# Two-layer hybrid diffusion trunk on one core: low parts of the choice stages on VectorE, attention two heads side by side

## The chip, the cores and the metric

The kernel runs on 1 core of one Trainium2 chip. The metric is the device time of one execution in microseconds (us). TensorE (PE) multiplies, VectorE (DVE), ScalarE (ACT) and GpSimd (POOL) work on the data between the multiplications, SyncE (SP) starts most transfers. All five run their own queue of instructions in order, and a semaphore holds an instruction until what it reads is there.

## The reference, cut to what matters

```
def reference(x, c, ctx, c_ctx, ...):
    lat, cx = x, ctx                                  # 256 latent and 256 context tokens, D = 1024
    for l in range(2):
        hl, hc = modulate(rms_norm(lat, ...)), modulate(rms_norm(cx, ...))
        yl, yc = even_mixer(...) if l % 2 == 0 else odd_mixer(...)
        lat = lat + gate * yl
        ff = peer(modulate(rms_norm(lat, ...)), w_q, b_q, sub_keys, u, v)   # layer 0: latent and context tokens
        lat = lat + gate * ff
    return lat

def sink_attention(q, k, v, sink, mask):              # in odd_mixer: 12 query heads of width 64, 4 key/value heads
    s = einsum(q, k) * 64 ** -0.5                     # 256 queries, 256 context keys and a window of latent keys
    p = softmax(concat([sink, where(mask, s, -inf)]))[..., 1:]
    return einsum(p, v)

def peer(h, w_q, b_q, sub_keys, u, v):                # per token, 8 heads
    q = h @ w_q + b_q                                 # 8 heads x 2 halves x 128
    s = einsum(q, sub_keys)                           # 128 keys for each half
    sv, si = top_k(s, 16)                             # for each half
    best, pos = top_k(sv[0][:, None] + sv[1][None], 16)
    gate, eidx = softmax(best), index of the pair     # 16 of 128*128 experts for each head
    act = gelu(einsum(h, u[eidx])) * gate
    return einsum(act, v[eidx])
```

All arithmetic is held to float32. The kernel gets there on the fast matmul type (fp32r) by splitting both operands into a high part (a copy rounded to fp32r) and a low part (the operand less its high part), with three matmuls for each product: high by high, high by low, low by high (`mm3`, L109, L110, L111).

## The kernel before, in words

The program is, for each of two layers, a mixer and an expert stage, run one after the other. Tile pools with a number of buffers for each tag carry the dependences; a scheduler of the tile framework orders the instructions of each engine's queue (outside the blocks ordered by hand, which lie in the dense stages and the first norm). What the order of the text says is thus not the order in a queue; the sections on order below show the queues.

**Mixer of layer 1** (about 1716 to 1871 us of the trace). Queries and keys of all heads are normalised and rotated by `heads` (L1062 on, buffers `hsq` and `hn`), transposed into `qt` (12 heads, two to a column of 128 partitions, 64 partitions each) and `kt` (four key heads, each on 64 of the 128 partitions, the other 64 rows zero, L1061 and L1115). For each head and half of the queries, `scores` (L1147 on) is one matmul of 128 x 512 over 128 rows (L1152; half of the rows are zeros in `kt`), a mask, a softmax on DVE and ACT; `flip` transposes the result (L1174) into `pt`; `values` (L1184 on) multiplies by `vt` into 64 columns of the array, four matmuls for each head (L1189), eight for a pair, of which the first four go to one half of the columns and the last four to the other. Scores run one step ahead of the transposes. Between these stand the modulation vectors of the same layer, `mod` (L161): groups of matmuls of which each uses 32 columns (L171).

**Expert stage** (`peer`, L499 on). A norm, then the choice of experts: for each of four blocks of `w_q` (two heads each) `wsplit` (L681 on) makes four high parts on ACT (L65) and four low parts (L73), three of them on POOL and the last on DVE, after the letters "ap ap ap av" (a = ACT, p = POOL, v = DVE). `evaluate` projects (L109 to L111, into `qp`), copies (L652), multiplies with the keys (L655, L661) and copies the scores out (`sc`, L657). `select` is DVE's: the two best eights of each 128 scores (L523 to L529), sums of pairs (L540, L543), the two best eights again (L549 to L555), the subtraction of the best (L557), then indices and a gather by comparison (L562 to L577). The softmax over all chosen ones (L581 to L585) ends the stage; its first instruction, an Exp on ACT (L581), needs L557 of the last head.

PE has room in this stage, and it is filled with the **first halves** of the dense stage after it: `spare(1)` after each head (L690) loads a block of `u`, makes its high part on ACT (L743) and its low part (`ul`, L748), multiplies (L109 to L111 into `mm`), applies a Gelu (L766) and stores the result. `prepare` and `spare` take the engine of the low part as an argument, POOL by default (L600 and L608). After the last head `spare(nq)` makes 2 more in layer 0 and 6 more in layer 1 (L694). Then come the gate-build (L789 to L820) and the dense loops, where the low parts are DVE's already. In the trace the choice of layer 0 lies at about 367 to 553.5 us (first selection at 399.5), that of layer 1 at about 1871 to 2003 us (first selection at 1895.4), and six first halves of layer 1 up to 2020.3 us.

Of the kernel before, what the change touches and what calls it, by code (L numbers as in the profile page):

```python
# [9 lines left out]
F32 = mybir.dt.float32  # L10
# [27 lines left out]
class Kern:  # L38
# [460 lines left out]
    def peer(self, l, halves, D0, nstash=0, nq=2, ng=(1, 1)):  # L499
# [11 lines left out]
        with ExitStack() as st:  # L511
# [107 lines left out]
            with ExitStack() as st2:  # L619
# [419 lines left out]
    def mixer1(self):  # L1039
        nc, i = self.nc, self.i  # L1040
        with ExitStack() as st:
            m = self.open(st, "m1")
            px = self.open(st, "m1ps", space=PSUM)
            aux = lambda shape: px(shape, F32, tag="aux", bufs=3)
            pj = lambda shape: px(shape, F32, tag="pj", bufs=3)
# [17 lines left out]
            def heads(x, nh, gain, out, rope):  # L1063
# [7 lines left out]
                n = m([128, nh, 64], F32, tag="hn", bufs=1)  # L1071
# [76 lines left out]
            def scores(c, o, t):  # L1148
                hd = 2 * c + o
                sk = rows[:, 128 + hd:129 + hd]  # L1150
                sp = pj([128, 512])
                nc.tensor.matmul(sp, qt[:, c, t * 128:(t + 1) * 128], kt[:, QPERM[hd] // 3], start=True, stop=True)  # L1152
                ob = 256 + (1 - t) * 128
                nc.vector.tensor_add(sp[:, ob:ob + 128], sp[:, ob:ob + 128], band[:, t])
                mx = m([128, 4], F32, tag="mx", bufs=4)
                nc.vector.tensor_reduce(mx[:, 0:1], sp, axis=AX.X, op=ALU.max)

                nc.vector.tensor_scalar(mx[:, 1:2], mx[:, 0:1], 0.125, sk, op0=ALU.mult, op1=ALU.max)
                nc.vector.tensor_scalar(mx[:, 1:2], mx[:, 1:2], -1.0, None, op0=ALU.mult)
                nc.scalar.activation(mx[:, 3:4], sk, AF.Exp, bias=mx[:, 1:2])  # L1160
                s = m([128, 512], F32, tag="s", bufs=3)
                nc.scalar.activation(s, sp, AF.Exp, bias=mx[:, 1:2], scale=0.125, accum_out=mx[:, 2:3])
                nc.vector.tensor_add(mx[:, 2:3], mx[:, 2:3], mx[:, 3:4])
                nc.vector.reciprocal(mx[:, 2:3], mx[:, 2:3])
                if t:
                    nc.vector.tensor_scalar(s, s, mx[:, 2:3], None, op0=ALU.mult)
                else:
                    nc.scalar.activation(s, s, AF.Copy, scale=mx[:, 2:3])
                return s
# [10 lines left out]
            steps = [(c, o, t) for c in range(6) for o in range(2) for t in range(2)]  # L1180
            S = {0: scores(*steps[0])}
            PT, OV = {}, {}

            def values(c, o):  # L1184
                kvh = QPERM[2 * c + o] // 3
                if o == 0:
                    OV[c] = self.mm([128, 256])
                for j in range(4):
                    nc.tensor.matmul(OV[c][64 * o:64 * o + 64], vt[:, j, 64 * kvh:64 * kvh + 64], PT[c][:, o, j], start=j == 0, stop=j == 3)  # L1189
                if o == 1:  # L1190
                    self.split(OV.pop(c), yh[:, c], yl[:, c])
                    for _ in range(2 if c in (1, 3) else 1):
                        self.mod(1, mods.pop(0))

            for n, (c, o, t) in enumerate(steps):
                if n + 1 < len(steps):
                    S[n + 1] = scores(*steps[n + 1])
                if (o, t) == (0, 0):
                    PT[c] = m([128, 2, 4, 256], F32, tag="pt", bufs=2)
                flip(S.pop(n), PT[c][:, o], t)  # L1200
                if t == 0 and n:
                    values(*steps[n - 1][:2])
# [117 lines left out]
```

## Time and profile before

| | us |
|---|---|
| median of 3 runs | 2738.8 (2738.1 to 2743.56) |
| the profiled execution, its own time | 2737.01 |
| its span in the trace | 2735.2 |
| PE busy | 2601.4 (95% of the span) |
| DVE busy | 2130.2 (78%) |
| ACT busy | 1382.1 (51%) |
| POOL busy | 656.0 (24%) |

Times of the trace are from the start of the span. What lies around the span is 1.8 us. "Busy" is the time in which an engine has an instruction in work, overlap counted once; a matmul's end is modelled, so a busy PE need not be at its peak. Shares of the whole span say little of a stage; the stages are looked at one by one, and in each the question is which engine has no idle time left, and what the others wait for. PEclk is the clock that TensorE was granted, as a share of 2.4 GHz.

### The profile page before, as it was taken

The page shows a single profiled execution, that of the slowest core. Times are in us where ns is not written, and L with a number is a line of the kernel's source. Part 1 is how long each engine was busy: PE and PEld are TensorE (multiplying, and loading weights), DVE is VectorE, ACT ScalarE, POOL GpSimd, SP SyncE. Part 2 cuts the span into 40 slices and gives each one's busy share as a digit, 9 for nine tenths or more (in the row PEclk, how much of TensorE's full clock was granted, in tenths as well). Part 3 has the DMA queues.
Part 4 walks back from the last instruction along what each step waited for, and adds up shares of the span by engine and source line. Part 5 has one row for each costly group of instructions (what it writes and reads, how often), then busy time and mean ns, then how long its engine had stood idle before and what let it go on. Part 6 is the DMA issues. An engine that isn't in the chain of part 4 may idle for free.

```text
span 2735.2 us, 40202 instructions
## 1 busy us (share of the span) xinstructions
PE 2601.4 (95%) x14788; PEld 2246.1 (82%) x14788; DVE 2130.2 (78%) x4518; ACT 1382.1 (51%) x2658; POOL 656.0 (24%) x573
## 2 busy tenths in 40 slices
PE   6999999999999999999999998998978999999998
PEld 4677777889999999988998997647868988888887
DVE  4678649999888787787877876655978788888886
ACT  4756543377544444444444435455356555555554
POOL 0000022288322222222222221104365011121220
PEclk9999999999999999999999999999989999999999
DMA  6333224345788888788878882255236889898993
GB/s 264 129 139 114 103 95 163 134 188 231 297 297 312 291 303 309 276 324 297 294 283 318 310 305 102 88 199 193 102 128 251 330 327 359 323 357 323 379 364 141
DMA packets 160036, 666.29 MB, mean 244 GB/s; under 512 B 11744, under 2 KB 87264, under 8 KB 87776
## 3 DMA queue, kind: packets, MB, share of 16 engines
q1 hardware_dynamic: 132192, 462.39, 46.2%
q0 software_dynamic: 27648, 201.34, 19.7%
q8 instruction: 117, 1.92, 0.3%
q14 instruction: 79, 0.65, 0.1%
HBM read 617.81 MB, written 45.88 MB: 243 GB/s over the span
## 4 chain that ended last, share of the span: by engine, by line
PE 61%; DVE 9%; ACT 2%; issue 1%; POOL 1%; DMA 0%; ACTq 0%; POOLq 0%; DVEq 0%
PE mm L111 9%; PE mm L110 9%; PE mm L109 9%; PE t L111 8%; PE t L110 8%; PE t L109 8%; PE gp L817 2%; PE t L938 2%; PE t L939 1%; DVE t L870 1%; DVE uv L854 1%; DVE vl L929 1%; DVE ul L748 1%; PE mm L1189 1%; PE pj L1152 1%
## 5 line engine op out<-in xcount | busy, mean ns | idle before, releaser
L109 PE MATMUL mm<-t,uh 128*128 128x384 f32 (+1 forms) x2048 | 632.3, 309 | 24.4 <-ACT c L766 24.0
L111 PE MATMUL mm<-t,ul 128*128 128x384 f32 (+1 forms) x2048 | 634.8, 310 | 21.3 <-DVE ul L748 19.4
L110 PE MATMUL mm<-t,uh 128*128 128x384 f32 (+1 forms) x2048 | 633.2, 309 | 0.0
L848 POOL DMA_INDIRECT uv<-in_uv_dram,t x192 | 316.4, 1648 | 1195.7 <-DVE t L870 1097.6
L109 PEld LDWEIGHTS mm<-t,uh 128*128 128x128 f32 x2048 | 394.3, 193 | 34.5 <-ACT c L766 25.1
L111 PEld LDWEIGHTS mm<-t,ul 128*128 128x128 f32 x2048 | 394.3, 193 | 25.5 <-DVE ul L748 22.8
L110 PEld LDWEIGHTS mm<-t,uh 128*128 128x128 f32 x2048 | 393.9, 192 | 10.7 <-issue 1.2
L110 PE MATMUL t<-vl,ch 128*128 128x512 f32 x1024 | 400.6, 391 | 0.5 <-DVE vl L929 0.5
L109 PE MATMUL t<-vh,ch 128*128 128x512 f32 x1024 | 401.1, 392 | 0.0
L743 ACT ACTIVATE uh<-r 128x1024 fp32r<-128x1024 f32 x256 | 270.3, 1056 | 242.1 <-PE mm L110 219.5
L971 ACT ACTIVATE ch<-c 128x384 fp32r<-128x384 f32 (+1 forms) x256 | 115.8, 453 | 547.2 <-PE t L110 187.9
L748 DVE TENSOR_TENSOR ul<-r,uh 128x1024 fp32r<-128x1024 f32 x230 | 280.7, 1221 | 82.9 <-ACT uh L743 82.7
L929 DVE TENSOR_TENSOR vl<-r,vh 128x1024 fp32r<-128x1024 f32 x256 | 312.0, 1219 | 0.0
L111 PE MATMUL t<-vh,cl 128*128 128x512 f32 x768 | 299.6, 390 | 0.0
L925 ACT ACTIVATE vh<-r 128x1024 fp32r<-128x1024 f32 x256 | 267.4, 1044 | 0.0
L870 DVE SCALAR_TENSOR_TENSOR t<-uv,act,t 128x1024 f32<-128x1024 f32 x190 | 242.4, 1276 | 5.4 <-ACT act L859 5.3
L854 DVE SCALAR_TENSOR_TENSOR uv<-uv,t 128x1024 f32<-128x1024 f32 x192 | 234.0, 1219 | 6.8 <-DMA uv<-in_uv_dram,t 6.8
L109 PEld LDWEIGHTS t<-vh,ch 128*128 128x128 f32 x1024 | 194.6, 190 | 37.0
L110 PEld LDWEIGHTS t<-vl,ch 128*128 128x128 f32 x1024 | 194.1, 190 | 36.6 <-DVE vl L929 0.9
L748 POOL TENSOR_TENSOR ul<-r,uh 128x1024 fp32r<-128x1024 f32 x26 | 65.5, 2522 | 599.5 <-PE mm L192 365.7
L815 POOL TENSOR_SCALAR o<-t,trs 128x128 f32<-128x128 f32 x288 | 194.9, 696 | 31.0 <-ACT trs L794 31.0
L975 DVE TENSOR_TENSOR cl<-c,ch 128x384 fp32r<-128x384 f32 x128 | 71.2, 556 | 146.5 <-ACT ch L971 146.5
(339 smaller groups left out, 4872.2 us busy)
## 6 DMA issues: line engine op xcount, KB each, us to landing
r<-in_ut_dram SPq DMA_DIRECT2D x128, 1024.0 KB, 7.3
r<-in_vv_dram SPq DMA_DIRECT2D x128, 1024.0 KB, 6.7
r<-in_wm_dram SPq DMA_DIRECT2D x48, 1024.0 KB, 5.2
t<-buf SPq DMA_DIRECT2D x18, 2048.0 KB, 7.4
gates<-t SPq DMA_DIRECT2D x48, 768.0 KB, 7.6
r<-in_wq_dram SPq DMA_DIRECT2D x16, 1024.0 KB, 5.1
r<-in_ew_dram SPq DMA_DIRECT2D x14, 1024.0 KB, 5.0
r<-in_ow_dram SPq DMA_DIRECT2D x6, 1024.0 KB, 4.9
```

The source lines that it names most:

```text
L109: mm(p, a[0], b[0], start=first, stop=False)
L110: mm(p, a[0], b[1], start=False, stop=False)
L111: mm(p, a[1], b[0], start=False, stop=last)
L743: nc.scalar.activation(uh, t[:, x], AF.Copy)
L748: (eng or nc.vector).tensor_tensor(u[1], u[2], u[0].bitcast(F32), op=ALU.subtract)
L815: nc.gpsimd.tensor_scalar(o1, self.iota, trs[:, 0, tk:tk + 1], None, op0=ALU.is_equal)
L848: nc.gpsimd.indirect_dma_start(out=UV[e], out_offset=None, in_=i[f"uv{l}"], in_offset=bass.IndirectOffsetOnAxis(ap=EI[:, e:e + 1], axis=0))
L854: nc.vector.scalar_tensor_tensor(x[:, 0:1024], x[:, 0:1024], 1.0, htok, op0=ALU.mult, op1=ALU.mult, accum_out=a)
L870: nc.vector.scalar_tensor_tensor(dacc, x, a, dacc, op0=ALU.mult, op1=ALU.add)
L925: nc.scalar.activation(vh, v, AF.Copy)
L929: nc.vector.tensor_tensor(x[1], x[2], x[0].bitcast(F32), op=ALU.subtract)
L971: nc.scalar.activation(x[0], C[n], AF.Copy)
```

## The change

It has four parts.

1. The low parts of the first halves made in the choice stages go from POOL to DVE: the default engine of `prepare` and `spare` is now VectorE.
2. The low parts of `w_q` go from POOL to DVE as well: `wsplit` is called with its default, "av" for all four.
3. Attention is written for pairs of heads. The scores of a pair are two matmuls of 64 rows each, one on rows 0 to 63 of the array, one on rows 64 to 127, next to each other in the text, into two banks. The values of a pair alternate between the two halves of the columns, j by j. Scores of both heads run one step ahead.
4. Buffers in that mixer: `aux` 3 to 2, `pj` 3 to 4 (PSUM), `s` 3 to 4; `hn` takes the buffer of `hsq`.

```diff
-            def prepare(eng=nc.gpsimd):
+            def prepare(eng=nc.vector):
...
-            def spare(n, eng=nc.gpsimd):
+            def spare(n, eng=nc.vector):
...
-                        w = self.wsplit(i[f"wq{l}"][b], mq, "ap ap ap av", bufs=5 if l == 0 else 8)
+                        w = self.wsplit(i[f"wq{l}"][b], mq, bufs=5 if l == 0 else 8)
...
-            aux = lambda shape: px(shape, F32, tag="aux", bufs=3)
-            pj = lambda shape: px(shape, F32, tag="pj", bufs=3)
+            aux = lambda shape: px(shape, F32, tag="aux", bufs=2)
+            pj = lambda shape: px(shape, F32, tag="pj", bufs=4)
...
-                n = m([128, nh, 64], F32, tag="hn", bufs=1)
+                n = m([128, nh, 64], F32, tag="hsq", bufs=1)
...
-            def scores(c, o, t):
-                hd = 2 * c + o
...
-                sp = pj([128, 512])
-                nc.tensor.matmul(sp, qt[:, c, t * 128:(t + 1) * 128], kt[:, QPERM[hd] // 3], start=True, stop=True)
...
-                s = m([128, 512], F32, tag="s", bufs=3)
...
+            def scores(c, t):
+                S = []
+                sp = [pj([128, 512]) for _ in range(2)]
+                for o in range(2):
+                    r = slice(64 * o, 64 * o + 64)
+                    nc.tensor.matmul(sp[o], qt[r, c, t * 128:(t + 1) * 128], kt[r, QPERM[2 * c + o] // 3], start=True, stop=True)
+                for o in range(2):
...
+                    s = m([128, 512], F32, tag="s", bufs=4)
...
+                    S.append(s)
+                return S
...
+            def values(c):
+                ov = self.mm([128, 256])
+                for j in range(4):
+                    for o in range(2):
+                        kvh = QPERM[2 * c + o] // 3
+                        nc.tensor.matmul(ov[64 * o:64 * o + 64], vt[:, j, 64 * kvh:64 * kvh + 64], PT[c][:, o, j], start=j == 0, stop=j == 3)
...
-            steps = [(c, o, t) for c in range(6) for o in range(2) for t in range(2)]
+            steps = [(c, t) for c in range(6) for t in range(2)]
...
+                for o, x in enumerate(S.pop(n)):
+                    flip(x, PT[c][:, o], t)
                 if t == 0 and n:
-                    values(*steps[n - 1][:2])
-            values(5, 1)
+                    values(c - 1)
+            values(5)
```

What this makes of the queues is shown at three places. The first is DVE's queue at the start of the choice of layer 0, between the norm's last instructions (L217) and the first selection (L523); the names are the tiles, `wlo` the low parts of `w_q`, `ul` those of the first halves.

```order
 L217 SCALAR_TENSOR_TENSOR t_2571<-xn_2709,t_87,t_2570 128x256
 L217 SCALAR_TENSOR_TENSOR t_2571<-xn_2713,t_87,t_2570 128x256
+L73 TENSOR_TENSOR wlo_2749<-r_2744,whi_2748 128x1024
+L73 TENSOR_TENSOR wlo_2753<-r_2744,whi_2752 128x1024
+L73 TENSOR_TENSOR wlo_2757<-r_2746,whi_2756 128x1024
 L73 TENSOR_TENSOR wlo_2761<-r_2746,whi_2760 128x1024
+L748 TENSOR_TENSOR ul_3050<-r_2838,uh_3049 128x1024
 L523 MAX sv_2764<-sc_2797 128x8 x2
```

Three low parts of the first block, and one of a first half, now stand in DVE's queue ahead of the first selection.

The second is DVE's queue in the choice of layer 1, behind the first head's index work (L565 to L577).

```order
+L748 TENSOR_TENSOR ul_17362<-r_17184,uh_17361 128x1024
 L568 CAST abf_17323<-ab_17317 128x32
 L573 TENSOR_TENSOR eq_17327<-abf_17323,t_16965 128x512
 L576 TENSOR_TENSOR eq_17327<-eq_17327,sif_17324 128x512
 L577 TENSOR_REDUCE t_16964<-eq_17327 128x2x16
+L73 TENSOR_TENSOR wlo_17691<-r_17686,whi_17690 128x1024
 L523 MAX sv_17222<-sc_17253 128x8
+L73 TENSOR_TENSOR wlo_17695<-r_17686,whi_17694 128x1024
 L524 MAX_INDEX si_17223<-sv_17222,sc_17253 128x8
 L527 MATCH_REPLACE s_17459<-sv_17222,sc_17253 128x128
+L73 TENSOR_TENSOR wlo_17699<-r_17688,whi_17698 128x1024
 L528 MAX sv_17222<-s_17459 128x8
```

The low parts of the next block and of one first half now stand between the selections, so that a selection behind them waits for whatever they wait for.

The third is PE's queue in the attention: a stretch before, with scores L1152, transposes L1174, values L1189 and modulation L171 and L180,

```order
L1152 MATMUL pj_16197<-t_15403,t_15405 128x512
L180 MATMUL mm_16148<-t_85,modm_16146 128x2 x4
L1174 MATMUL aux_16167<-t_68,s_16115 128x128 x4
L1152 MATMUL pj_16216<-t_15403,t_15405 128x512
L1189 MATMUL mm_16192<-pt_16120,t_15404 64x256 x2
L1174 MATMUL aux_16186<-t_68,s_16162 128x128 x4
L1189 MATMUL mm_16192<-pt_16120,t_15404 64x256 x2
L171 MATMUL mm_16246<-r_16242,t_89 32x512
L1174 MATMUL aux_16210<-t_68,s_16181 128x128 x4
```

and a stretch of the changed kernel, where these lines are L1153, L1179 and L1190.

```order
L1153 MATMUL pj_16186<-t_15403,t_15405 128x512
L180 MATMUL mm_16180<-t_85,modm_16178 128x2 x4
L1153 MATMUL pj_16187<-t_15403,t_15405 128x512
L1179 MATMUL aux_16212<-t_68,s_16125 128x128 x4
L1179 MATMUL aux_16218<-t_68,s_16136 128x128 x4
L1153 MATMUL pj_16224<-t_15403,t_15405 128x512
L1153 MATMUL pj_16225<-t_15403,t_15405 128x512
L1190 MATMUL mm_16263<-pt_16141,t_15404 64x256 x8
L171 MATMUL mm_16278<-r_16274,t_89 32x512
```

The two matmuls of a pair of scores stand side by side in 7 of the 12 steps, as the second pair here does; in the other 5 something stands between them, as L180 in the first. Values of a pair mostly come in one run of eight.

## Rows read from the trace of the kernel before

**Rows 1.** By stretch: length, busy PE, PEld, DVE, ACT, POOL, then PEclk, DMA share, GB/s.
```profile
399.50:533.00 133.50, 133.50 (x683) 105.32 (x682) 129.06 (x595) 42.94 (x72) 36.18 (x15) 1.00 0.35 128
533.00:553.50 20.50, 14.89 (x92) 12.70 (x92) 20.19 (x91) 8.17 (x11) 5.60 (x2) 0.97 0.49 184
...
1748.60:1844.00 95.40, 89.88 (x443) 45.66 (x443) 58.50 (x196) 44.95 (x113) 2.24 (x2) 0.98 0.43 155
...
1895.40:1985.00 89.60, 83.50 (x644) 75.48 (x643) 85.58 (x320) 39.53 (x88) 35.92 (x15) 1.00 0.33 118
1985.00:2003.00 18.00, 2.04 (x8) 1.80 (x9) 17.56 (x70) 4.09 (x6) 4.16 (x2) 0.62 0.04 5
```

**Rows 2.** Costliest groups of the page: the low parts on DVE and POOL.
```profile
L748 DVE TENSOR_TENSOR ul<-r,uh 128x1024 fp32r<-128x1024 f32 x230 | 280.7, 1221 | 82.9 <-ACT uh L743 82.7
...
L748 POOL TENSOR_TENSOR ul<-r,uh 128x1024 fp32r<-128x1024 f32 x26 | 65.5, 2522 | 599.5 <-PE mm L192 365.7
```

**Rows 3.** Groups on DVE, 1895.3 to 2003: line, operation, count | busy us, mean ns.
```profile
L576 DVE TENSOR_TENSOR eq<-eq,sif 128x1024 bf16<-128x1024 bf16 x4 | 6.7, 1680 | 0.1
...
L523 DVE MAX8 sv<-sc 128x8 f32<-128x128 f32 x16 | 4.5, 283 | 6.8 <-ACT sc L657 6.8
L543 DVE TENSOR_TENSOR cand<-sv 128x16 f32<-128x16 f32 x4 | 4.5, 1128 | 0.0
...
L543 DVE TENSOR_TENSOR cand<-sv 128x8 f32<-128x8 f32 x4 | 4.1, 1032 | 0.0
...
L557 DVE TENSOR_TENSOR t<-best 128x16 f32<-128x16 f32 x4 | 3.6, 893 | 0.0
```

**Rows 4.** Timeline from 1905 us: start, duration, engine, line.
```profile
1905.26 7.06 POOL L73 TENSOR_TENSOR wlo<-r,whi 128x1024 fp32r<-128x1024 f32 x3 [1.00 <-ACT whi L65]
...
1907.67 2.33 DVE L563 TENSOR_SCALAR b<-pos 128x16 uint32<-128x16 uint32 x1
```

**Rows 5.** Single lines on DVE, 399.5 to 553.5: shortest/median/longest in ns.
```profile
L543 DVE TENSOR_TENSOR cand<-sv x8: 160/165/1776, 409.9 to 540.8; 128x24 f32<-128x24 f32 x8
...
L557 DVE TENSOR_TENSOR t<-best x8: 189/192/2211, 414.6 to 545.3; 128x48 f32<-128x48 f32 x8
...
L576 DVE TENSOR_TENSOR eq<-eq,sif x8: 937/957/2644, 419.1 to 548.5; 128x1536 bf16<-128x1536 bf16 x8
```

**Rows 6.** Who waited for whom (total us, times, longest), 389 to 560.
```profile
PE qp L111 <- POOL wlo L73: 2.7, 3, 1.6
```

**Rows 7.** The same, 1880 to 1900.
```profile
PE qp L111 <- POOL wlo L73: 3.9, 3, 2.1
```

**Rows 8.** Timelines of PE and of ACT where the two choice stages end.
```profile
553.11 0.87 PE L789 MATMUL mm<-t,t 128*128 128x128 f32 x3 [4.89 <-DVE t L577]
...
1997.46 0.36 ACT L581 ACTIVATE t<-t 128x192 f32<-128x192 f32 x1 [16.11 <-DVE t L557]
```

**Rows 9.** Timeline of DVE, selections of the last head of layer 0.
```profile
536.08 0.29 DVE L528 MAX8 sv<-s 128x8 f32<-128x128 f32 x1
536.40 0.09 DVE L529 MATCH_VALUE_LOAD si<-sv,s 128x8 f32 x1
...
536.68 0.47 DVE L523 MAX8 sv<-sc 128x8 f32<-128x128 f32 x2
```

**Rows 10.** Timelines of ACT and of DVE in the choice of layer 0, 495 to 499.
```profile
495.87 2.01 ACT L65 ACTIVATE whi<-r 128x1024 fp32r<-128x1024 f32 x2 [0.68 <-DMA r<-in_wq_dram]
...
497.87 0.28 DVE L527 MATCH_REPLACE8 s<-sv,sc 128x128 f32<-128x128 f32 x1
```

**Rows 11.** Timeline of PE in the attention: start, duration of the run, line, count.
```profile
1774.44 1.98 PE L1152 MATMUL pj<-t,t 128*128 128x512 f32 x4
...
1785.01 1.94 PE L1189 MATMUL mm<-pt,t 128*64 128x256 f32 x8
...
1790.15 1.92 PE L171 MATMUL mm<-r,t 128*32 128x512 f32 x16
```

**Rows 12.** The values' line in the attention: shortest/median/longest in ns, count.
```profile
L1189 PE MATMUL mm<-pt,t x96: 379/379/431, 1764.8 to 1849.2; 128*64 128x256 f32 x96
```

More of the change, by code (lines that the diff above doesn't have):

```diff
@@ new lines, in scores @@
+            def scores(c, t):
[5 more added lines that the diff above has]
+                for o in range(2):
+                    hd, p = 2 * c + o, sp[o]
+                    sk = rows[:, 128 + hd:129 + hd]
+                    ob = 256 + (1 - t) * 128
+                    nc.vector.tensor_add(p[:, ob:ob + 128], p[:, ob:ob + 128], band[:, t])
+                    mx = m([128, 4], F32, tag="mx", bufs=4)
+                    nc.vector.tensor_reduce(mx[:, 0:1], p, axis=AX.X, op=ALU.max)
+                    nc.vector.tensor_scalar(mx[:, 1:2], mx[:, 0:1], 0.125, sk, op0=ALU.mult, op1=ALU.max)
+                    nc.vector.tensor_scalar(mx[:, 1:2], mx[:, 1:2], -1.0, None, op0=ALU.mult)
+                    nc.scalar.activation(mx[:, 3:4], sk, AF.Exp, bias=mx[:, 1:2])
+                    s = m([128, 512], F32, tag="s", bufs=4)
+                    nc.scalar.activation(s, p, AF.Exp, bias=mx[:, 1:2], scale=0.125, accum_out=mx[:, 2:3])
+                    nc.vector.tensor_add(mx[:, 2:3], mx[:, 2:3], mx[:, 3:4])
+                    nc.vector.reciprocal(mx[:, 2:3], mx[:, 2:3])
+                    if t:
+                        nc.vector.tensor_scalar(s, s, mx[:, 2:3], None, op0=ALU.mult)
+                    else:
+                        nc.scalar.activation(s, s, AF.Copy, scale=mx[:, 2:3])
+                    S.append(s)
+                return S
@@ L1178, in flip @@
                     nc.scalar.activation(pt[:, :, t * 128:(t + 1) * 128], p, AF.Copy)
-            steps = [(c, o, t) for c in range(6) for o in range(2) for t in range(2)]
-            S = {0: scores(*steps[0])}
[L1182 to L1195, printed above, removed]
+            def values(c):
[4 more added lines that the diff above has]
+                        nc.tensor.matmul(ov[64 * o:64 * o + 64], vt[:, j, 64 * kvh:64 * kvh + 64], PT[c][:, o, j], start=j == 0, stop=j == 3)
+                self.split(ov, yh[:, c], yl[:, c])
+                for _ in range(2 if c in (1, 3) else 1):
+                    self.mod(1, mods.pop(0))
+            steps = [(c, t) for c in range(6) for t in range(2)]
+            S = {0: scores(*steps[0])}
+            PT = {}
+            for n, (c, t) in enumerate(steps):
                 if n + 1 < len(steps):
                     S[n + 1] = scores(*steps[n + 1])
-                if (o, t) == (0, 0):
+                if t == 0:
                     PT[c] = m([128, 2, 4, 256], F32, tag="pt", bufs=2)
-                flip(S.pop(n), PT[c][:, o], t)
+                for o, x in enumerate(S.pop(n)):
+                    flip(x, PT[c][:, o], t)
                 if t == 0 and n:
-                    values(*steps[n - 1][:2])
-            values(5, 1)
+                    values(c - 1)
+            values(5)
             for b in range(2):
```

16 lines of the change are left out of this document (removed).

## The prediction

> **What bounds the kernel now.** I read the busy time by stretch first, then who waits for whom at both ends of each stretch, then the durations on VectorE (DVE), and last TensorE's (PE's) timeline in the attention. The change touches three stretches, and each has its own limit.
>
> Choice of layer 0, 399.5 to 553.5 us: PE and DVE are both nearly full, PE at 133.5 of 133.5 and DVE at 129.06, and in the last 20.5 us DVE at 20.19 while PE has only 14.89 [rows 1]. The end is DVE's: PE waits 4.89 us for DVE's last reduction before it can start the gate-build [rows 8]. A microsecond added to DVE here comes out at the end.
>
> Choice of layer 1, 1895.4 to 2003: DVE is busy 85.58 of 89.6 and then 17.56 of 18, while PE has done nearly all it can and works 2.04 us of the last 18, at a granted clock of 0.62 [rows 1]. ACT's Exp, which waited 16.11 us for DVE's L557 of the last head, is what lets the rest of the program go on [rows 8]. So again DVE, but here with nothing of PE beside it.
>
> Attention, 1748.6 to 1844: PE is busy 89.88 of 95.4, DVE only 58.50, ACT 44.95 [rows 1]. Here PE sets the time.
>
> One thing is hidden in DVE's busy time. While POOL works on low parts from 1905.26 on, for 7.06 us, an instruction of 16 elements a partition (L563) takes 2.33 us on DVE [rows 4]. The same is seen in groups: L543 has a mean of 1128 and 1032 ns in layer 1 [rows 3], although its larger form in layer 0 has a median of 165 ns [rows 5]. The selections themselves (L523, 283 ns) show nothing of it [rows 3]. So some of DVE's time is waiting for POOL, and moving POOL's work over to DVE both adds and takes away there.
>
> **The change part by part.** *The price of a moved low part.* One takes 1.22 us on DVE and 2.52 on POOL [rows 2]. Of the 50 that move, the queues show where each one stands; those which stand ahead of the first selection lie in DVE's idle time and are free. Behind it stand 17 in layer 0 (9 of the weights, 8 of first halves) and 14 in layer 1 (7 and 7).
>
> *Choice of layer 0.* Added to DVE: 17 x 1.22 = +20.7. Taken away, the waits for POOL: L557 has 8 x 192 = 1.5 us of its own, and its 5.6 us (8 x its mean of 0.70) hold 4.1 more; one L576 took 2644 instead of 957 ns, one L543 1776 instead of 165 [rows 5]; together -7.4. Start: PE waited 2.7 us in total for POOL's low parts in three steps [rows 6]; with 1.2 us instead of 2.5 for each that goes, and the first selection comes as much earlier: -2.7. Then a credit that I can only bound. An instruction of DVE that follows one on the same data starts 0.32 us after it (536.08 to 536.40), two on different data start some 0.19 us apart (0.47 for two, each 0.28) [rows 9]. In the changed queue the selections are mixed more with other work, and neighbours on the same tile fall from 223 to 157: 66 x 0.13 = 8.6 at most, and none if they stood where something else was waited for. I take 6, since DVE is full. Sum: 20.7 - 7.4 - 2.7 - 6 = +4.6, **taken as +4**, from -3 (the same with all of the credit, and a PE that ends earlier too) to +11 (no credit).
>
> What can stand before DVE here: the moved low parts need ACT's high parts, and the slack is small. The weights' high parts of the last block ended at 497.88 on ACT, and the place of the low parts in DVE's new queue corresponds to 497.87 in the old one [rows 10]. Of the 17 places I lined up this way, 6 have less than 1 us of slack. DVE's neighbours in the queue then wait too, and PE behind them. This is the third rival; at the forecast I count nothing for it, since DVE comes to these places later than before by what is added to it.
>
> *Choice of layer 1.* Added: 14 x 1.22 = +17.1. Taken away: the eight L543, 4 x (1.13 - 0.16) + 4 x (1.03 - 0.16) = 7.4; four L557, 4 x (0.89 - 0.19) = 2.8; four L576, 4 x (1.68 - 0.64) = 4.2, with 0.64 as two thirds of the 0.957 of the larger form [rows 3, 5]; single long ones in L563 (2.33 instead of 0.17) and, of like size, in L569, L565 and L540, together 7.7 [rows 4]. That is about 22, of which some 2 lie behind the Exp: -20. Start: PE waited 3.9 us for POOL in three steps [rows 7]: -3.9. Mixing: 11 fewer same-tile neighbours, -1.4 at most. Sum 17.1 - 20 - 3.9 - 1.4 = -8.2, **taken as -9** with a little for the clock, which PE would not lose for so long (0.62 in that stretch [rows 1]). Bounds -14 (with the queue mixing as in layer 0) and -4 (PE is then the limit: it has 83.50 of the 89.6 us to work [rows 1], so that its own pace allows only the start and little else).
>
> *The six first halves behind it.* Their low parts cost 1.22 instead of 2.52 [rows 2], but the first of them now stands behind the last head's index work (L562 to L577) on DVE. One against the other: **0**, within 2.
>
> *Attention.* Scores: 48 records, four of them in 1.98 us; a single one is about as long as one of L171, 0.59, so the spacing is (1.98 - 0.59)/3 = 0.46 and all take 22 us. Values: eight in 1.94 us, one 0.38 [rows 11, 12], so (1.94 - 0.38)/7 = 0.22 each, and 96 take 21.4 us. They use half of the array's columns each, those of one head one after the other. That matmuls on separate columns run beside each other is shown by L171: 16 of them, four groups of 32 columns, take 1.92 us [rows 11], where 16 in a row at 0.46 would take 7.4. By this row alternated values take half: -10.7. For separate rows the trace has no case. The lower bound is nothing, the upper half the time for the 7 of 12 pairs that stand side by side: 22 x 7/12 / 2 = -6.4. Together 0 to -17. I take **-13**: nearest to the row of L171, which stands for the larger part, and less than all since PE then has some 77 us to work in a stretch in which scores, DVE, ACT and transposes hang on each other step by step, with two PSUM buffers for transposes instead of three.
>
> A thing that speaks against it: the first matmul of a run of values takes 431 ns instead of 379 [rows 12]. The 12 pairs of scores on half of the rows make up to 24 more such changes, 24 x 0.05 = 1.2 us, and it is in the -13. The Trainium skill, "TensorEngine Tiling (Array Packing)", section "Key Properties", states that a change of tiling mode drains TensorE; by that the price of a change would be a whole pipeline and not 52 ns, an estimate of 24 x 0.4 = 10 us from the single records above, and the sum of the attention would come to about -4. No row here shows a drain of this size around L171 or L1189, which change the mode dozens of times.
>
> The buffer shared by `hsq` and `hn` makes the second group's square wait until the first one's rotation has read; DVE has 58.50 of 95.4 us to do there [rows 1], so I count 0, within 1.
>
> *Sum:* +4 - 9 + 0 - 13 = -18. The profiled execution took 2737.0 us; 2737 - 18 = **2719**. The median of the runs stands 1.8 above the profiled one, which is less than what the terms leave open.
>
> **The rivals.** *First: the attention gives nothing.* Rows of the array don't work beside each other, or the pairs wait for DVE and ACT instead of PE (DVE's and ACT's work is strung along each step). Or every change of the array's shape costs a matmul's length, 24 x 0.38 = 9 us, of the gain (what the skill's rule would make of it). For it: no case of separate rows in the trace, and 5 pairs are split. Against it: L171, and 431 against 379 ns. Time: 2737 + 4 - 9 = 2732, with the second mechanism alone 2728; of its 0.15 the rule has 0.04.
>
> *Second: PE limits the choice of layer 1*, so that only -4 comes of it. For it: 83.50 of 89.6. Against it: PE's 2.04 us in the last 18 show that it had finished long before. Time: 2737 + 4 - 4 - 13 = 2724.
>
> *Third, slower: DVE stands waiting ahead of the moved low parts.* In POOL's queue a wait for ACT or for a buffer that PE holds cost nobody else; in DVE's it holds the selections. Price: 1.5 us on each of the 31 in the two stages, +46, so 2737 - 18 + 46 = 2765. It decides from 18/31 = 0.6 us for each. For it: the slack of 0 at 497.9 [rows 10]. Against it: in layer 1 the first halves' high parts are ready some 10 us ahead of their places.
>
> *Fourth, better:* values and scores both halve (-17), and in layer 0 all of the credit is there (-3): 2737 - 3 - 9 - 17, about 2708, or a little less.
>
> **How the numbers follow.** Forecast 2719, 0.55, with a range of its own of 2711 to 2727; first rival 0.15; second 0.13; third 0.07; fourth 0.10. A difference under 0.2%, 5.5 us, can't be told from no change, so 2733.3 to 2744.3 counts as the same. The first rival's 2732 lies at that bound, and I give half of it to each side: faster 0.55 + 0.13 + 0.10 + 0.08 = 0.86, the same 0.07, slower 0.07. The range for 8 in 10 leaves out the third rival and the far ends of the others: 2703 to 2732.
>
> **What would show it.** Right: L543, L557 and L563 at their short durations in layer 1; the Exp some 8 to 13 us earlier, measured from the end of the mixer; PE's wait before L789 still for DVE; eight values in about 1.1 us and a side-by-side pair of scores in about one's time; the attention some 13 us shorter. Wrong: idle DVE time ahead of L73 or L748 for ACT (third rival), PE without gaps up to the end of the choice of layer 1 (second), pairs of scores one after the other, or waits of PE for DVE and ACT in the attention (first).

## The result, and the profile after

The changed kernel takes 2717.55 us (median of 4 runs, 2716.38 to 2720.7) against 2739.14 for the kernel before: a ratio of 0.9922, 95% interval 0.991 to 0.9935. The forecast was 2719. The profiled execution took 2717.4 us, with a span of 2715.2 against 2735.2.

Where the 20.0 us of span went, read from marks that both traces have: the first selection of each choice stage (L523), the copy with which each gate-build begins (L794), the first reduction of `heads` (L1068) and the end of the last addition of the output projection in the mixer. The last column is what the prediction's terms had for it.

| stretch | before | after | difference | predicted |
|---|---|---|---|---|
| start to first selection, layer 0 | 399.5 | 396.0 | -3.5 | -2.7 |
| first selection to gate-build, layer 0 | 154.5 | 160.3 | +5.8 | +7.3 (taken as +6.7) |
| gate-build and dense loops of layer 0, norm of the mixer | 1151.4 | 1151.4 | 0 | 0 |
| first reduction of `heads` to the mixer's end | 166.0 | 155.6 | -10.4 | -13 |
| mixer's end to first selection, layer 1 | 24.0 | 21.4 | -2.6 | -3.9 |
| first selection to the Exp | 102.1 | 95.5 | -6.6 | -4.3 (taken as -5.1) |
| Exp to gate-build (first halves) | 22.8 | 21.8 | -1.0 | 0 |
| rest | 714.9 | 713.3 | -1.6 | 0 |

Single executions shift by a microsecond or two in the mixer of layer 0: the first selection of layer 0 came between 395.97 and 398.08 in the twelve kernels of this document that have the low parts of its first block on VectorE, at 396.8 in their mean. So stretches are compared by their lengths, and of the -3.5 in the first row -2.7 is the better figure.

The busy times by stretch of the changed kernel, in the columns of [rows 1] (length, PE, PEld, DVE, ACT, POOL, PEclk, DMA share, GB/s):

```profile
1750.90:1836.00 85.10, 79.50 (x440) 40.37 (x440) 59.50 (x197) 44.15 (x113) 2.63 (x2) 0.92 0.45 170
...
1884.60:1968.00 83.40, 78.07 (x599) 70.26 (x597) 80.14 (x339) 37.82 (x85) 0.00 (x0) 1.00 0.40 134
1968.00:1984.00 16.00, 6.25 (x48) 5.56 (x46) 15.66 (x66) 5.57 (x9) 0.00 (x0) 0.75 0.01 2
...
396.00:533.00 137.00, 135.19 (x680) 105.95 (x680) 133.55 (x618) 42.53 (x72) 0.00 (x0) 0.99 0.35 125
533.00:556.00 23.00, 15.57 (x97) 13.22 (x95) 22.76 (x85) 8.66 (x12) 0.00 (x0) 0.93 0.45 164
```

POOL has left both choice stages, and DVE is the engine without idle time in both: 133.55 of 137.0 and 22.76 of 23.0 in layer 0, 80.14 of 83.4 and 15.66 of 16.0 in layer 1. In the attention PE has 79.50 us to work instead of 89.88.

The durations on DVE in layer 1 (shortest/median/longest in ns), to be read against [rows 3, 4]:

```profile
L543 DVE TENSOR_TENSOR cand<-sv x8: 147/154/161, 1891.1 to 1977.3; 128x8 f32<-128x8 f32 x4, 128x16 f32<-128x16 f32 x4
```
```profile
L557 DVE TENSOR_TENSOR t<-best x8: 156/164/177, 1893.0 to 1979.9; 128x16 f32<-128x16 f32 x4, 128x32 f32<-128x32 f32 x4
```
```profile
L563 DVE TENSOR_SCALAR b<-pos x8: 167/172/179, 1893.2 to 1980.1; 128x16 uint32<-128x16 uint32 x4, 128x32 uint32<-128x32 uint32 x4
```

L543 had means of 1128 and 1032 ns; now none is longer than 161. L557, with a mean of 893 in its smaller form, takes 177 at most. L563's 2.33 us are gone, its longest is 0.18.

Who waits at the two ends now, and what DVE waits for, in the answer on who waited for whom (total us, times, longest) for 385 to 558, and below it for 1863 to 2003:

```profile
PE mm L789 <- DVE t L577: 6.7, 1, 6.7
...
DVE ul L748 <- ACT uh L743: 1.0, 1, 1.0
...
DVE wlo L73 <- ACT whi L65: 0.5, 1, 0.5
```
```profile
DVE ul L748 <- ACT uh L743: 10.8, 6, 4.4
ACT t L581 <- DVE t L557: 10.2, 1, 10.2
...
DVE wlo L73 <- ACT whi L65: 2.4, 3, 1.0
```

PE's wait for DVE at the end of layer 0 grew from 4.89 to 6.7 us [rows 8], the Exp's wait in layer 1 fell from 16.11 to 10.2. DVE stands before moved low parts for 1.5 us in layer 0, all of it ahead of the first selection. (The 10.8 us of layer 1 lie behind the Exp, in the six first halves, where ACT in turn waits for PE.)

And PE's timeline in the attention (start, duration of the run, line, form, count):

```profile
1782.66 1.12 PE L1153 MATMUL pj<-t,t 64*128 64x512 f32 x2
1783.71 1.05 PE L180 MATMUL mm<-t,modm 128*128 128x2 f32 x8
1784.69 1.12 PE L1153 MATMUL pj<-t,t 64*128 64x512 f32 x2
1785.75 1.09 PE L1179 MATMUL aux<-t,s 128*128 128x128 f32 x8
1786.77 1.13 PE L1153 MATMUL pj<-t,t 64*128 64x512 f32 x4
1787.83 2.42 PE L1190 MATMUL mm<-pt,t 128*64 128x256 f32 x16
```

A pair of scores in a row (four records, two for each matmul) holds PE from 1786.77 to 1787.83, 1.06 us; one head alone (two records) from 1782.66 to 1783.71, 1.05 us. So the two run beside each other fully. But a pair that is split costs 2.1 us, more than the 1.82 that four records took before (1774.44 to 1776.26). Sixteen records of values take 2.35 us, not the 1.9 that a half would be.

### The profile page after: what moved, and what is told of

The parts are those of the page before. It is cut to its first block, busy times and chain, and to the rows that moved or that the text cites. A ratio compares the mean times of both kernels' runs of the same rounds, so it can differ in the third digit from the quotient of the medians.

```text
span 2715.2 us, 40194 instructions
## 1 busy us (share of the span) xinstructions
PE 2588.8 (95%) x14788; PEld 2236.2 (82%) x14788; DVE 2147.9 (79%) x4568; ACT 1381.9 (51%) x2658; POOL 531.6 (20%) x523
## 4 chain that ended last, share of the span: by engine, by line
PE 51%; issue 13%; DVE 4%; POOL 3%; ACT 1%; DMA 1%; POOLq 0%; ACTq 0%; DVEq 0%
PE mm L111 7%; PE mm L110 7%; PE mm L109 7%; PE t L111 7%; PE t L110 7%; PE t L109 7%; POOL uv L848 3%; PE gp L817 1%; DMA uv<-in_uv_dram,t 1%; PE pj L1153 1%; PE mm L171 1%; PE t L938 1%; PE t L939 1%; PE pj L111 1%; PE pj L109 1%
## 5 line engine op out<-in xcount | busy, mean ns | idle before, releaser
L111 PE MATMUL mm<-t,ul 128*128 128x384 f32 (+1 forms) x2048 | 633.0, 309 | 22.6 <-DVE ul L748 22.5
L109 PE MATMUL mm<-t,uh 128*128 128x384 f32 (+1 forms) x2048 | 630.6, 308 | 17.5 <-ACT c L766 16.8
L110 PEld LDWEIGHTS mm<-t,uh 128*128 128x128 f32 x2048 | 392.7, 192 | 10.7 <-issue 1.2
L748 DVE TENSOR_TENSOR ul<-r,uh 128x1024 fp32r<-128x1024 f32 x256 | 312.7, 1222 | 77.9 <-ACT uh L743 77.6
L111 PEld LDWEIGHTS t<-vh,cl 128*128 128x128 f32 x768 | 144.2, 188 | 30.5
```

The lines of the kernel that those rows point to most:

```text
L109: mm(p, a[0], b[0], start=first, stop=False)
L110: mm(p, a[0], b[1], start=False, stop=False)
L111: mm(p, a[1], b[0], start=False, stop=last)
L748: (eng or nc.vector).tensor_tensor(u[1], u[2], u[0].bitcast(F32), op=ALU.subtract)
```

## The experiments

All times are medians; beside each stands the ratio to the kernel before on the same chip, with its 95% interval. The kernel before had medians of 2738.4 to 2739.9 in these comparisons. "Mixer" is the stretch from the first reduction of `heads` to the mixer's end in the run's trace, 166.0 us before and 155.6 in the changed kernel. These lengths come from one execution each; the same attention took 154.6 to 155.6 in four traces, so differences under 1 us mean little.

### The two halves of the change, apart

The choice stages alone: the first three hunks of the change.

```diff
-            def prepare(eng=nc.gpsimd):
+            def prepare(eng=nc.vector):
-            def spare(n, eng=nc.gpsimd):
+            def spare(n, eng=nc.vector):
-                        w = self.wsplit(i[f"wq{l}"][b], mq, "ap ap ap av", bufs=5 if l == 0 else 8)
+                        w = self.wsplit(i[f"wq{l}"][b], mq, bufs=5 if l == 0 else 8)
```

> The choice stages of the change alone: all low parts on VectorE in both layers, the attention and its buffers as before. My theory, with the stretches measured in the changed kernel (layer 0 ends 2.2 us later, layer 1 starts its selections 2.6 us earlier, works 6.7 us less, first halves 1 us less): 2739 - 8 = 2731. By the terms of the prediction (+4 and -9) 2734. Rival: the two halves of the change help each other (a shorter mixer is what makes the choice of layer 1 start sooner), so that this one alone is worth 3 us or less: 2736 or more.

Measured: 2729.64 us, 0.9968 (0.9955 to 0.998); the mixer takes 166.0 us. The attention alone is the rest of the diff.

> The attention of the change alone, with its buffers; low parts on GpSimd as before. My theory, from the stretch between the first scores and the last projection, which went from 122.6 to 112.3 us: 2739 - 10 = 2729; the prediction's own term was -13, 2726. Rival: part of the 10 us comes from the choice stages' changed queues, and less than 7 is left: 2732 or more.

Measured: 2727.56 us, 0.9961 (0.9947 to 0.9975). The gains are 8.8 and 10.8 us (against the kernel before of the same chip, 2738.39), 19.6 together, and the change's own is 21.6: they add, within what such runs can tell. Neither rival holds.

### Does VectorE wait for GpSimd?

The changed kernel, with useless subtractions on GpSimd in the choice of layer 1, as many and at the same places as its work before. It computes the same and does work that nobody reads. (The operands are shortened here.)

```diff
                     ready[waits[k]] = part(waits[k], eng)
+                    if l and idle[0]:
+                        nc.gpsimd.tensor_tensor(dum, hh_part, uh, op=ALU.subtract)
...
+                            for x in range(3):
+                                nc.gpsimd.tensor_tensor(dum, hh_part, hi[x], op=ALU.subtract)
```

> The changed kernel, and in the choice of layer 1 GpSimd makes as many subtractions of the same size as before the change, at the same places (each waits for the high part that it waited for before), into a tile that nobody reads. So VectorE has the moved work and GpSimd's work beside it. My theory: VectorE's short operations with two inputs wait for GpSimd again, some 20 us: 2717.5 + 20 = 2737, with the mean of L543 near 1000 ns again. Rival: the gain of that stage comes from TensorE and VectorE no longer waiting for GpSimd's results; then nothing waits for the copies and the time stays 2717.5, with L543 at 160 ns.

Measured: 2752.33 us, 1.0046 (1.0028 to 1.0065). That is 35 us more than the changed kernel, not 20, though nobody needs these copies. (Only ACT waits for them, 3.6 us in all, before two of its high parts.) Before the first selection stand five low parts of the query weights on DVE; first in the changed kernel, then here, in DVE's timelines (start, duration, line):

```profile
1878.89 5.77 DVE L73 TENSOR_TENSOR wlo<-r,whi 128x1024 fp32r<-128x1024 f32 x5 [0.95 <-ACT whi L65]
```
```profile
1879.39 15.62 DVE L73 TENSOR_TENSOR wlo<-r,whi 128x1024 fp32r<-128x1024 f32 x5 [0.95 <-ACT whi L65]
```

And POOL's timeline beside the latter:

```profile
1877.26 10.06 POOL L697 TENSOR_TENSOR dum<-t,whi 128x1024 fp32r<-128x1024 f32 x3 [121.30 <-ACT whi L65]
1887.40 6.52 POOL L613 TENSOR_TENSOR dum<-t,uh 128x1024 fp32r<-128x1024 f32 x2
```

The same five instructions take 15.62 us beside POOL's and 5.77 without: 3.1 us each instead of 1.15. POOL's own take 3.3 each, where they had a mean of 2.52 [rows 2]. In the selections that follow (1894.9 to the Exp at 2013.7) the stretch is 23.3 us longer than in the changed kernel. Some of its groups on DVE (the lines of the selection are 2 higher here; count | busy us, mean ns):

```profile
L73 DVE TENSOR_TENSOR wlo<-r,whi 128x1024 fp32r<-128x1024 f32 x11 | 17.6, 1599 | 0.0
...
L578 DVE TENSOR_TENSOR eq<-eq,sif 128x512 bf16<-128x512 bf16 x4 | 5.8, 1460 | 0.1
...
L525 DVE MAX8 sv<-sc 128x8 f32<-128x128 f32 x16 | 4.5, 280 | 0.0
...
L570 DVE CAST abf<-ab 128x32 bf16<-128x32 uint32 x4 | 2.9, 727 | 0.1
```

The multiplication L578 of this form had a mean of 425 ns in the changed kernel (there L576), the cast L570 had 180 (L568), and the maximum keeps its 0.28. Summed from each start to the next, the comparisons and multiplications L575 and L578 take 10.5 us more than in the changed kernel, the casts L570 4.4, the subtraction L559 2.5, the additions L567 and L542 3.5, and the low parts 3.5. Within this trace, too, the two of L578 that run beside POOL's work take 2.5 us each, the two others of this form 0.43. So what the theory said of the cause is shown: POOL's work alone, with no result that anybody needs, makes DVE's operations with two inputs wait; the casts, with one input, wait as well, the maxima don't. What it said of the place was wrong: L543 (L545 here) stayed at 154 and 145 ns, since the work fell beside other instructions. And the sum was too small, because the moved low parts are themselves such operations: they cost 9.8 us ahead of the first selection and the 3.5 behind it.

### Layer 0 back on GpSimd, but for the first block

```diff
-            def prepare(eng=nc.vector):
+            low = nc.vector if l else nc.gpsimd
+            def prepare(eng=low):
...
-                        w = self.wsplit(i[f"wq{l}"][b], mq, bufs=5 if l == 0 else 8)
+                        w = self.wsplit(i[f"wq{l}"][b], mq, "ap ap ap av" if l == 0 and b else "av av av av", bufs=5 if l == 0 else 8)
```

> The changed kernel, but in the choice of layer 0 all low parts go back to GpSimd, save those of the first block of query weights, which stay on VectorE. My theory: in layer 0 VectorE sets the end, and the move added 20.7 us to it and took 7.6 us of waiting and 7 us of gaps away; only the first block's low parts helped (first selection 3.5 us earlier). So 2.2 + 3.5 = 5.7 us are gained: 2717.5 - 5.7 = 2711.8. Rival: TensorE, as busy there as VectorE, sets the end then, and 2 us or less are gained: 2715.5 or more.

Measured: 2710.45 us, 0.9895 (0.988 to 0.991): 7.1 us better than the changed kernel. From the first selection to the gate-build it takes 154.3 us, as before (154.5), while the first selection keeps its earlier start (396.6). So in layer 0 the move itself was a loss, and only the first block's part of it a gain. The rival that PE sets the end there falls.

### What the attention's gain is made of

Four kernels take the changed attention apart. First, scores over all 128 rows again:

```diff
-                    nc.tensor.matmul(sp[o], qt[r, c, t * 128:(t + 1) * 128], kt[r, QPERM[2 * c + o] // 3], start=True, stop=True)
+                    nc.tensor.matmul(sp[o], qt[:, c, t * 128:(t + 1) * 128], kt[:, QPERM[2 * c + o] // 3], start=True, stop=True)
```

> The changed kernel, but the two scores of a pair are again multiplied over all 128 rows (half of them zeros); values still alternate between the two halves of the columns. My theory: in the changed kernel 7 pairs stand side by side and take 1.06 us each, 10 single ones take 1.05 each, 17.9 us; over 128 rows one takes 0.91, 21.8 for all. So 3.9 us are lost: 2717.5 + 3.9 = 2721.4. Rival: rows of 64 are worth their full half, or nothing: 2728, or 2717.5.

Measured: 2714.96 us, 0.9909 (0.9892 to 0.9925); mixer 151.1 us. That is no loss; by the trace the mixer is 4.5 us shorter than the changed kernel's. My theory failed here. Then the values head by head, with the scores on 64 rows:

```diff
-                for j in range(4):
-                    for o in range(2):
+                for o in range(2):
+                    for j in range(4):
```

> The changed kernel, but the values of a pair are multiplied head by head again, four matmuls on one half of the columns and then four on the other. My theory: sixteen records at 0.147 us instead of 0.234, six pairs, 8.3 us are lost: 2717.5 + 8.3 = 2725.8, less if VectorE and ScalarE hide some. Rival: values hang on their transposes and the alternation is worth under 3 us: 2720.5 or less.

Measured: 2722.15 us, 0.9941 (0.9924 to 0.9957); mixer 158.9 us. A loss of 4.6 us instead of 8.3. Then both of these edits together, so that nothing is written to run side by side:

> The changed kernel with neither side-by-side form: scores over all 128 rows and values head by head; what is left of the attention's change is that pairs go through together, one step ahead, and the buffers. Theory: alternating the values is worth the 9.5 us of TensorE that they fell by with columns only (23.07 to 13.54), so 2715.0 + 9.5 = 2724.5, and the pairs and buffers some 4 us of the gain. Rival: pairs and buffers are worth nothing, 2728.5; or most of it, 2719 or less.

Measured: 2718.99 us, 0.9923 (0.9906 to 0.9939); mixer 154.3 us. That is the changed kernel's time, within the runs, without either side-by-side form. And last the buffers alone, on the choice stages' kernel, heads one by one as before:

```diff
-            aux = lambda shape: px(shape, F32, tag="aux", bufs=3)
-            pj = lambda shape: px(shape, F32, tag="pj", bufs=3)
+            aux = lambda shape: px(shape, F32, tag="aux", bufs=2)
+            pj = lambda shape: px(shape, F32, tag="pj", bufs=4)
-                n = m([128, nh, 64], F32, tag="hn", bufs=1)
+                n = m([128, nh, 64], F32, tag="hsq", bufs=1)
-                s = m([128, 512], F32, tag="s", bufs=3)
+                s = m([128, 512], F32, tag="s", bufs=4)
```

> The kernel before with the choice stages of the change, and of the attention's change the buffers alone (aux 2, pj 4, s 4, hn in the buffer of hsq); heads still go through one by one. It stands between the choice stages alone (2729.6) and pairs with buffers but nothing alternated (2719.0). Theory: the 10.6 us between them come from pairs: both heads' values stand together in the queue, so that the second head's run beside the first's tail (16 records in 2.79 us instead of 3.74), and TensorE's queue changes less often between forms. Then buffers alone change little: 2729.6, within 2. Rival: the fourth buffers for scores and softmax are what lets TensorE run on: 2722 or less.

Measured: 2727.47 us, 0.9956 (0.9939 to 0.9972); mixer 164.0 us. So the steps of the mixer's length are: 166.0 with the choice stages alone, 164.0 with the buffers, 154.3 with pairs, 151.1 with alternated values, and 155.6 with scores on 64 rows as well, which is the changed kernel. Pairs are worth 9.7 us, the alternation 3.1, the buffers 2, the rows cost 4.5; by the runs the last is 2.6 (2717.55 against 2714.96). Pairs without the added buffers weren't run. Nor was it tested apart that with pairs the scores of two heads run ahead instead of one head's.

Why pairs alone gain can be read from PE's queue. Before, the values of one head stood alone between other work, and the modulation's groups of four were cut; PE's timeline of the kernel before, 1782 to 1788:

```profile
1782.45 1.05 PE L171 MATMUL mm<-r,t 128*32 128x512 f32 x2
1783.43 0.66 PE L1174 MATMUL aux<-t,s 128*128 128x128 f32 x4
1784.02 1.06 PE L171 MATMUL mm<-r,t 128*32 128x512 f32 x8
```

Two records of L171 hold PE for 0.98 us there (1782.45 to 1783.43), and eight for no more (1784.02 to 1785.01). With pairs, L171 takes 16.8 us for its 128 records instead of 20.8 (sums from each start to the next, without PE's idle time), transposes 11.9 instead of 12.6, values 17.5 instead of 23.1, and the values go through in 9 runs instead of 16. PE's idle time from the first scores to the last values is 4.3 us instead of 5.4. The values gain although they stand head by head: PE's timelines of the pairs alone, and then of the columns only:

```profile
1783.46 2.86 PE L1190 MATMUL mm<-pt,t 128*64 128x256 f32 x16
1786.25 1.05 PE L171 MATMUL mm<-r,t 128*32 128x512 f32 x2
```
```profile
1785.01 1.95 PE L1190 MATMUL mm<-pt,t 128*64 128x256 f32 x16
1786.88 1.04 PE L171 MATMUL mm<-r,t 128*32 128x512 f32 x2
```

Sixteen records, eight of each head, take 2.79 us one head after the other, 1.87 alternated; before, eight took 1.87 [rows 11]. When the second head's stand directly behind the first's, on the other half of the columns, part of them runs beside: 2.79 against the 3.74 of twice eight. Alternated, it is half.

### Why 64 rows lose

Three things cost there. Going from 128 rows to 64 and back costs time: a run of eight transposes before a score holds PE for 1.02 us with 64 rows (1785.75 to 1786.77 above) and 0.87 with 128, and one head alone 1.05 instead of 0.86. Behind a pair the two halves of the columns start 0.48 us apart, so that sixteen records of values take 2.35 instead of 1.87. And the clock: in the mean over 15 us, the windows of PE's idle time and the matmuls behind it, of the kernel before, the changed one and the one with columns only (columns as in [rows 1]):

```profile
1753.00:1768.00 15.00, 14.40 (x58) 9.88 (x59) 10.84 (x35) 6.70 (x18) 0.00 (x0) 0.89 0.00 1
```
```profile
1753.00:1768.00 15.00, 11.17 (x24) 6.50 (x24) 9.32 (x25) 3.79 (x11) 2.39 (x2) 0.54 0.01 1
```
```profile
1755.00:1770.00 15.00, 10.65 (x40) 7.59 (x40) 12.81 (x37) 5.39 (x16) 2.63 (x2) 0.89 0.01 1
```

The granted clock is 0.54 in the changed kernel, 0.89 in the other two. Looked at microsecond by microsecond it is at its lower level of 1.2 GHz for 3.4 us before (1753.9 to 1757.3, behind an idle time of PE of 3.8 us) and for 13.7 us in the changed kernel (1754.1 to 1767.8, from within one of 4.4 us), through transforms (L1138, L1144) that are the same in all three. In PE's timelines of the kernel before and of the changed one, eight records of L1144 take twice as long:

```profile
1757.64 1.89 PE L1144 MATMUL aux<-t,t 128*128 128x256 f32 x8
```
```profile
1762.32 3.78 PE L1144 MATMUL aux<-t,t 128*128 128x256 f32 x8
```

The sums of PE from the first scores to the last values, of the changed kernel against columns only, say what each is worth: the scores themselves are 3.0 us shorter (19.4 against 22.4); the transforms and the transposes of the queries, which stand in the low clock, are 3.5 longer; transposes, values and L180, which border on the 64-row scores, 2.6 longer; and PE is idle for 1.3 us more. To tell the clock from the changes of shape, the first four steps' scores went back to 128 rows:

```diff
-                    r = slice(64 * o, 64 * o + 64)
+                    r = slice(64 * o, 64 * o + 64) if c > 1 else slice(0, 128)
```

> The changed kernel, with the scores of the first four steps over all 128 rows and those of the other eight on 64 rows. Theory: rows of 64 lose because the first ones stand where TensorE's clock has just fallen: its granted clock was 0.50 for some 13 us there in the changed kernel, 3.4 us before and with columns only. Away from there a pair side by side takes 1.06 us instead of 1.82, less 0.1 to 0.2 for each change of shape and 0.47 where values follow. So about 2714 to 2715, with the low clock for some 3.4 us only. Rival: the changes of shape themselves lose it, wherever they are: 2716.5 or more, with the clock low for 10 us or more all the same.

Measured: 2714.81 us, 0.9903 (0.9887 to 0.992); mixer 149.8 us, and the window from 1750 to 1765 has a mean clock of 0.77:

```profile
1750.00:1765.00 15.00, 12.35 (x43) 8.11 (x42) 12.53 (x33) 4.49 (x13) 2.24 (x2) 0.77 0.00 1
```

The low clock comes in two pieces of 3.4 us each, not in the one that was expected. The loss is gone, as the theory expected, and the rows away from there are a small gain over columns only by the trace (149.8 against 151.1), none by the runs: there the scores are 3.2 us shorter, and what borders on them is 2.2 longer. The transforms and the transposes of the queries are back at 7.1 us, from 10.5 in the changed kernel. By these sums the low clock makes the largest part of the loss. Why the low stretch is longer with early 64-row scores is not shown. But it is so in every trace: in the seven kernels of this document whose first scores are on 64 rows, one piece of 6.8 to 13.7 us follows them, and in the seven others no piece there is longer than 3.4 us.

### All pairs in a row

(Shortened; the two matmuls stand inside the raised priority.)

```diff
-                sp = [pj([128, 512]) for _ in range(2)]
+                pp = pair()                              # one tile of two banks, 2 buffers, for projections too
+                sp = [pp[:, 0], pp[:, 1]]
+                with self.tc.high_priority(100):
```

> The changed kernel, but the two scores of a pair are one tile of two banks, and issued with a raised priority, so that all 12 pairs stand side by side in TensorE's queue instead of 7. My theory: 5 pairs take 1.06 us instead of 2.1, -5.2 us: 2712.3. Rival: the later pairs wait for both banks, and VectorE and ScalarE are what the attention then waits for: between 2716 and 2720.

Measured: 2724.17 us, 0.9939 (0.9924 to 0.9954); mixer 161.4 us. It loses 6.6 us. The scores did fall to 14.1 us of PE from 19.4. But transposes took 14.5 instead of 12.7 and the modulation 19.1 instead of 15.9, cut into smaller runs again: a matmul that is drawn forward is paid for by those that it cuts. From the first scores to the last values it took 85.4 us, as in the changed kernel (85.5). The loss stands mostly ahead of that: the first scores came 47.4 us after the first reduction of `heads` instead of 43.3. The projections there share the two double buffers; that this is the cause is not shown. The rival's time was too low too.

> Both together: layer 0's low parts on GpSimd save those of the first block, and all pairs of scores side by side. If both theories hold the gains add: 2717.5 - 5.7 - 5.2 = 2706.6. With one of them alone 2712, with none 2717.

Measured: 2718.13 us, 0.9916 (0.9903 to 0.993). The layer-0 edit keeps its 6 us on top of the pair tile (2724.17), and loses 7.7 against the layer-0 edit alone.

### The best of the edits

Columns only, and layer 0 on GpSimd but for the first block:

> The two single edits that were faster than the changed kernel, together: scores over all 128 rows (columns still alternate), and layer 0's low parts on GpSimd save the first block. They lie in different stages; if they add: 2715.0 + 2710.45 - 2717.5 = 2708. Rival: the later program absorbs one of them: 2710.5.

Measured: 2707.06 us (2703.64 to 2708.68), 0.9877 (0.986 to 0.9893). It beats the kernel before by 1.2% and the changed kernel by 10.5 us; the gains add.

## Why the prediction was right, and where it wasn't

**Layer 0, taken as +4, measured +2.3** (+5.8 - 3.5; +3.1 with the mean start of -2.7). The addition was exact: DVE's time from each start to the next, summed by line, grew by 20.7 us for the 17 moved low parts. The waits for POOL gave back 6.8 (4.1 in L557, 2.0 in L576, 0.8 in L543) instead of 7.4. The rest, 8.1, is shorter steps between other instructions, which the prediction had as a credit of 6 with 8.6 as its bound; steps of some 0.32 us among the selections (L523 to L555) fell from 44 to 8, the others take some 0.20, which is 4.5 us of it. The sum is right for its reasons, and the experiment that takes the move back has the stage at its old length.

**Layer 1, taken as -9, measured -10.2.** The start gave 2.6 instead of 3.9. Between first selection and Exp, 15.9 us were added and 22.5 came off; the lines named for contention (L540, L543, L557, L563, L565, L569, L576) carry 20.4 of them, against the 20 of the prediction. The copy of POOL's work shows that the cause is POOL's work and not the wait for its results. The first halves gave 1.0, within the 2 that were left open.

**Attention, taken as -13, measured -10.4: the sum was near, the reason was wrong, and that they agree is in part luck.** The step that failed is the one that took the whole gain from matmuls side by side. It held everything else as it was: "they use half of the array's columns each, those of one head one after the other", so halved by alternating. The values did fall, from 23.1 us to 13.5 with columns only, nearly by the 10.7 of the prediction; but 5.6 of these 9.5 came already with the pairs, unalternated, together with 4.0 in the modulation, 0.6 in the transposes and 1.1 of PE's idle time, which the prediction did not look at. The scores were mis-sized: bounds of 0 and -6.4, taken as a few us; two matmuls on 64 rows run fully side by side, and yet the rows cost 4.5 in the mixer. The price of a change of shape, 0.05 us from [rows 12], was the wrong row: that row changes columns, and a change of rows costs some 0.1 to 0.15 us going in and 0.19 coming out. The Trainium skill, "TensorEngine Tiling (Array Packing)", section "Key Properties", states that a change of tiling mode drains TensorE; these 0.3 us for a stay on 64 rows are some 0.15 for each change, more than my 0.05 and less than the 0.4 estimated from a drain. The clock's longer low stretch stood in no term at all.

**The rivals.** That the attention gives nothing is refuted as a sum and holds for one half: what was written to run side by side, rows and columns together, is worth nothing in the runs (2718.99 against 2717.55), because the columns gain about what the rows lose. PE as the limit of layer 1: no, PE had 78.07 of 83.4 us to work and 6.25 of the last 16. DVE standing before the moved low parts: 1.5 us of waiting in layer 0 and 2.4 in layer 1, 1.4 of it ahead of the first selection, far from the 0.6 us for each of 31 from which it would have decided. The fourth, some 2708: layer 0 did get nearly all of its credit (8.1 of 8.6) and was slower all the same, and the attention stayed below its bound.

## What to carry to other kernels

Before moving work from one engine to another, look for instructions whose time depends on what the other engine does; the same move was worth 10 us in a stage where the short operations kept running into GpSimd's, and cost 6 in one where they rarely did, so decide it stage by stage. When code is rewritten so that matmuls run side by side, run the rewritten order without the side-by-side form too: here the order, with its buffers, gave as much as the whole change (2718.99 against 2717.55 us), in part because matmuls that stand together in it overlap without being alternated. A shape that is faster for itself can be paid for by its neighbours and by the clock, so it is read from the length of the stretch, not from its own rows.

## What the hardware showed that was not expected

- Subtractions on GpSimd and operations of two inputs on DVE slow each other: five on DVE took 15.62 us beside GpSimd's and 5.77 alone, and GpSimd's 3.3 us each instead of 2.52. A cast on DVE, with one input, had a mean of 727 ns instead of 180 there; the maxima kept their 280.
- Matmuls on separate halves of the columns overlap in part without being alternated, if they stand directly behind each other: sixteen records in 2.79 us against 2 x 1.87 apart and 1.87 alternated.
- Where the first scores were on 64 rows, the granted clock stood at 0.50 for 6.8 to 13.7 us in one piece behind them (seven traces); in the seven other traces no piece at that place was longer than 3.4, also where later scores were on 64 rows. The cause is open.
